# A planner that knows the delay between dependent neighbours, and convolution tiles placed after the following projection

## The chip, the cores and the metric

The kernel runs on one core of one Trainium2 chip. The metric is the device time of one execution in microseconds (us); lower is better. Five engines take part: TensorE (PE in the profile, its weight loads PEld), VectorE (DVE), ScalarE (ACT), GpSimd (POOL) and SyncE (SP, which only issues DMAs).

## The reference

A trunk of two layers over 512 tokens of width 1024, batch 1. Layer 0 mixes tokens with a gated linear recurrence and trailing means, layer 1 with a Conformer convolution module. Each layer then does cross-attention into 256 memory tokens and a gated MLP with a causal convolution of width 3. The change lies in layer 1's Conformer module and in the planner of the whole program:

```python
def conformer_conv(x, norm, w1, b1, dw_w, dw_b, ln_g, ln_b, w2, b2):
    h = rms_norm(x, norm) @ w1 + b1
    h = jax.nn.glu(h, axis=-1)
    h = causal_dwconv(h, dw_w, dw_b)
    h = jax.nn.silu(layer_norm(h, ln_g, ln_b))
    return h @ w2 + b2
```

`x` is 512 x 1024, `w1` 1024 x 2048, `w2` 1024 x 1024, all float32.

## The kernel before

Activations lie transposed, 128 channels on the partitions and 512 tokens along the free axis, so the width 1024 is eight tiles (`C = 8`). A float32 product is made of three matmuls in a reduced format (`mm3`, line 629): operands are split into a high and a low part (`split`, line 622: ACT copies the high part, DVE or POOL subtracts it), and a projection of one tile is 8 such triples, 24 matmuls of 128x512. A weight comes by an SP load into a 4 KB tile of the pool `w` (18 buffers) and is split into two more 4 KB tiles there, or, with `park=True`, into four 2 KB tiles of the pool `act` (48 buffers) (`load_w`, line 608).

**The planner.** No instruction is issued where it stands in the code. `Recorder` (line 201) collects every operation as a node with an estimated cost (`cost`, line 271), and `plan` (line 319) makes the order: first a backward pass (`late`, line 339) gives every node a due time, then a forward pass plays the engines and lets each take, whenever it is free, the first node that is ready: PE in program order, within a window of 60 nodes (`PE_WINDOW`), the others by due time. Buffers of the pools `act` and `w` go in the order of due times, those of the PSUM pools and of `tmp` in program order. The result is a fixed order for each engine and for SP's queue. A node on the same engine as the one it depends on is taken to be ready the moment that one ends; in the backward pass it is put down with the hop of another engine.

**The Conformer module** (`conformer`, line 1340). For each channel tile c: `project` with the second half of w1 gives the gate (ACT sigmoid, `gate`), `project` with the first half gives the value, and `gated` (line 1357) multiplies them on DVE into a buffer h (three of them in turn) and issues four SP DMAs that copy h into four `stacked` tiles, each with four shifted copies of 32 channels. `spread` (line 1369, POOL) prepares the filter taps as small matrices. `conv_pe` (line 1379) does the first taps of the convolution on PE, as float32 tiles of 128x32: 2 groups of 4 tiles for c = 0 to 6, 8 groups for c = 7. They accumulate in a PSUM buffer of the pool `aux`, of which there are two. `conv` (line 1396) adds the rest of the 31 taps: for c = 0 to 6 four on POOL (with ACT) and 19 on DVE, each a `scalar_tensor_tensor` that reads and writes the same PSUM buffer; c = 7 has none left. `merge` (line 1416) joins the parts with the bias and sets the PSUM buffer free.

In program order the loop's step c is: gate projection of tile c+1, `spread(c + 1)`, `conv_pe(c)`, value projection and `gated(c + 1)`, the weights of tile c+2, `conv(c)`. In the last step the attention's `mem.keys(4)` stands in the place of the gate projection. Behind the loop comes the layer norm over channels: sums over PE (`quarters`, `total`), squares, the root of the variance on ACT (`spread_scale`, line 767), then for each tile a multiply on DVE, Silu on ACT and a split. Work for the following cross-attention that needs nothing of this chain (`mem.values(0)`, `mem.values(1)`, `mem.keys(5)` to `mem.keys(7)`) stands behind it in program order, so PE can take it while it waits. Then `project_all` multiplies with the first three tiles of w2, loaded by `load_w(I["pw2"][n])`, all three side by side.

The feed-forward stages (line 978) take about half of the span. They are issued through the same planner; their code isn't touched.

Of the kernel before, what the change touches and what calls it, by code (L numbers as in the profile page):

```python
# [12 lines left out]
F32 = mybir.dt.float32  # L13
F32R = mybir.dt.float32r
AF = mybir.ActivationFunctionType
ALU = mybir.AluOpType

P = 128
# [3 lines left out]
C = D // P  # L22
# [14 lines left out]
PE_GROUPS = [2, 2, 2, 2, 2, 2, 2, 8]  # L37
N_POOL = [4] * 7 + [0]
LAG = 5
PLAIN = 3  # L40

KE = 4
# [140 lines left out]
class Node:  # L183

    def __init__(self, index, eng):
        self.index, self.eng, self.calls, self.us, self.tail = index, eng, [], 0.0, 0.0
        self.table, self.port, self.lat = None, False, 0.0
        self.before, self.after = set(), set()
        self.start = self.end = None


# [9 lines left out]
class Recorder:  # L201
# [4 lines left out]
    PATIENCE = 40.0  # L206
    WIRE = 0.83 / (256 * 1024)
    LAND = {"SP": 1.9, "ACT": 1.9, "POOL": 2.3}

    def __init__(self, tc):  # L210
        self.tc, self.nc = tc, tc.nc
# [35 lines left out]
    def touch(self, node, v, write):  # L247
        t = v.tile
        lo, hi, mask, _ = v.region()
        if t.psum:  # L250
            lo, hi, mask = 0, 127, 1
        if not t.nodes:
            self.tiles.append(t)
        if not t.nodes or t.nodes[-1] is not node:
            t.nodes.append(node)

        def meets(e):
            return e[0] <= hi and lo <= e[1] and e[2] & mask

        for e in t.writes + (t.reads if write else []):  # L260
            if meets(e) and e[3] is not node:
                node.before.add(e[3])
        if write:
            keep = lambda e: not (lo <= e[0] and e[1] <= hi and (e[2] & mask) == e[2])
            t.writes = [e for e in t.writes if keep(e)]
            t.reads = [e for e in t.reads if keep(e)]
            t.writes.append((lo, hi, mask, node))
        else:
            t.reads.append((lo, hi, mask, node))

    def cost(self, node, eng, method, args, how, reads):
        out = args[0]
        n = int(np.prod((reads[0] if not isinstance(out, View) else out).shape[1:]))
        if method == "dma_start":
            src = out if isinstance(out, View) else reads[0]
            node.tail += self.WIRE * 4 * n * src.shape[0] * (1.9 if "accum_op" in how else 1)
            window = any(k[0] == "window" for k in src.steps) or any(k[0] == "window" for r in reads for k in r.steps)
            node.us += 0.65 if window else {"SP": 0.42, "ACT": 0.42, "POOL": 0.6}[eng]
            return
        if eng == "PE":  # L280
            node.lat = 0.17
            if method == "transpose":
                node.us += 0.11
            elif out.shape[0] == 32:
                node.us += 0.875 / 4
            else:
                plain = args[1].tile.dtype == F32
                node.us += max(0.11, 0.0133 + n / 2400.0) * (4 if plain and n > 128 else 1)
            return
        wide = max([n] + [int(np.prod(r.shape[1:])) for r in reads[:1]])  # L290
        sources = [r for r in reads if int(np.prod(r.shape[1:])) > 4]
        node.port = node.port or eng == "POOL" and method != "memset"
        if eng == "ACT":
            node.lat = 0.1
            node.us += 0.1 + wide * 0.00083
            if isinstance(how.get("bias"), View):
                node.us += 0.06
            if "accum_out" in how:
                node.us += 0.2
            f = args[2]  # L300
            if f not in (AF.Copy, AF.Identity, AF.Square):
                node.table = f
        elif eng == "DVE":
            node.lat = 0.08
            node.port = node.port or len(sources) > 1 and not any(r.tile.psum for r in sources)
            if method == "reciprocal":
                node.us += 0.07 + wide * 0.00625
            elif method == "tensor_tensor_scan":
                node.us += 0.12 + wide * 0.002
            elif method == "scalar_tensor_tensor":  # L310
                node.us += 0.12 + wide * 0.00106
            else:
                node.us += 0.07 + wide * 0.001046
        else:
            node.lat = 0.06
            slow = method == "tensor_tensor" and how["op"] == ALU.mult
            node.us += 0.1 + n * (0.001 if method == "memset" else 0.0033 if slow else 0.0023)

    def plan(self):
# [19 lines left out]
        def late(extra):  # L339
            for o in reversed(nodes):  # L340
                due = end if o.ideal is None else o.ideal + o.us
                for a in list(o.after) + extra.get(o, []):
                    due = min(due, a.due - self.HOP - o.lat - (o.tail + self.LAND[o.eng] + self.SAFE if o.tail else 0.0))
                o.due = due - 1.15 * o.us

        def turn(t):
# [27 lines left out]
        ready = {e: [] for e in ("PE", "ACT", "DVE", "POOL", "SP")}  # L374
# [21 lines left out]
        while done < len(nodes):  # L396
# [11 lines left out]
            for e, r in ready.items():  # L408
# [4 lines left out]
                for i, (_, _, o) in enumerate(r):  # L413
# [21 lines left out]
                    us = o.us  # L435
# [15 lines left out]
                    del r[i]  # L451
                    done += 1
                    heapq.heappush(soon, (o.end, o.index, "end", o))
                    hop = lambda a: now + us if a.eng == o.eng and not o.tail else o.end + self.HOP
                    for a, at in [(a, hop(a)) for a in o.after] + [(a, now) for a in opens.get(o, [])]:
                        wait[a] -= 1
                        a.at = max(getattr(a, "at", 0.0), at)
# [52 lines left out]
def trunk(ctx: ExitStack, tc: tile.TileContext, I: dict, out_t: bass.AP, out: bass.AP):  # L510
# [23 lines left out]
    def nm(s):  # L534
        uid[0] += 1
        return f"{s}_{uid[0]}"
# [18 lines left out]

    def aux_ps():
        return aux.tile([P, T], F32, tag="aux", name=nm("aux"))

    wide = [True, 0]

# [21 lines left out]
    def col(name, i=0):  # L582
        j = _COL[name] + i
        return par[:, j : j + 1]
# [58 lines left out]
    class Norm:  # L643
        due = None
# [119 lines left out]
        V.reciprocal(r, sd)  # L764
        return r

    def spread_scale(s, weight):

        ps = stat_ps()
        for j in range(4):  # L770
            PE.matmul(ps[:, j : j + 1], s[:, j * P : (j + 1) * P], weight[:, :1], start=True, stop=True)
        rt = small.tile([P, 4], F32, tag="rtok", name=nm("rtok"), bufs=2)
        A.activation(rt, ps[:, :4], AF.Sqrt, bias=eps)
        V.reciprocal(rt, rt)
        d = tmp_f()
        V.tensor_tensor(
            d.rearrange("p (a b) -> p a b", a=4), ident.unsqueeze(1).broadcast_to([P, 4, P]),
            rt.unsqueeze(2).broadcast_to([P, 4, P]), op=ALU.mult,
        )
        out = aux_ps()  # L780
        PE.matmul(out, unit, d, start=True, stop=True)
        return out

    def project(w, i, xs):
        ps = mm_ps()
        for k in range(C):
            mm3(ps, blk(w, k * P), xs[k], k == 0, k == C - 1)
        if Norm.due:
            Norm.due.r = rstd(Norm.due.ss)
            Norm.due = None  # L790
        return ps
# [548 lines left out]
    def conformer(norm, nxt, mem, parked):  # L1340
        fold = small.tile([P, 32], F32, tag="fold", name="fold", bufs=1)
        V.tensor_reduce(fold, ident.rearrange("p (a b) -> p a b", b=4), axis=mybir.AxisListType.X, op=ALU.add)
        hs, outs = [None] * C, []

        def gate(c, psb):
            b = tmp_f()
            A.activation(b, psb, AF.Sigmoid, bias=col("c_b_pw1", C + c))
            return b

        def pieces(c):  # L1350
            return load_w(I["pw1"][C + c], V if c == 2 else G), load_w(I["pw1"][c], G)
# [84 lines left out]
        gated(0, gate(0, ps[0]), ps[1])  # L1436
        w = w[2:]
        mu = stat_ps()
        for c in range(C):
            if c < C - 1:  # L1440
                b = gate(c + 1, project(w[0], c + 1, norm.x))
                spread(c + 1)
            else:
                mem.keys(KE)
            conv_pe(c)
            if c < C - 1:
                gated(c + 1, b, project(w[1], c + 1, norm.x))
                if c < C - 2:
                    w = pieces(c + 2)
            else:  # L1450
                mem.eng = G
                ready = [mem.piece(i, park=True) for i in range(4)] + [mem.piece(i) for i in range(4, 8)]
            conv(c)
        merge(*pend.pop())
        mean = total(mu, aux_ps())
        var, sqs = aux_ps(), []
# [5 lines left out]
                quarters(var, sqs)  # L1462
        f = tmp_f()
        A.activation(f, var, AF.Copy)
        r = spread_scale(f, fourth)
        xs = []
        for c in range(C):
            V.tensor_tensor(outs[c], outs[c], r, op=ALU.mult)
            f = act_f()
            A.activation(f, outs[c], AF.Silu, scale=col("c_ln_g", c), bias=col("c_ln_b", c))  # L1470
            xs.append(split(f))
        mem.values(0, ready[:4])
        mem.values(1, ready[4:])
        for n in range(KE + 1, C):
            mem.keys(n)
        mem.eng = None

# [3 lines left out]
            V.scalar_tensor_tensor(X[n], ps, col("c_b_pw2", n), X[n], op0=ALU.add, op1=ALU.add)  # L1481
            nxt.feed(n)

        w = [load_w(I["pw2"][n]) for n in range(3)]
        for n, ps in enumerate(project_all(w, xs)):
            finish(n, ps)
        for n in range(3, C):
# [116 lines left out]
```

## Time and profile before

| | us |
|---|---|
| median of 3 runs | 1433.64 |
| lowest, highest | 1433.30, 1433.87 |
| the profiled execution's own time | 1433.83 |
| its span, first to last instruction | 1432.0 |
| PE busy in the span | 1421.8 |
| DVE busy | 1223.8 |
| ACT busy | 853.2 |
| POOL busy | 185.3 |

The granted clock of PE is 1.000 over the span. The Conformer module runs from about 735 to 910 us. Where the profile says that PE is busy, matmuls are in flight; a tile that waits inside a block shows in the length of the block more than in PE's idle time. All operations go through one line of the recorder, L498, so groups are told apart by their tiles' names: `mm`, `aux` and `stat` are PSUM buffers, `h` is the gated tile, `actf` a 2 KB tile, `wf` a raw weight, `wr` a 4 KB split operand, `tmp` a temporary. In a timeline row stand the start, the length of the merged row, the engine and the operation with its count, and in brackets the idle time before it and who ended it. Rows of one engine overlap by the pipeline's length, so the pace of a series is its length less that of one operation, over the count less one.

### The profile page before, as it was taken

The numbers are of one execution on the slowest core, as the hardware profiler recorded it, in microseconds if no ns is written. First come the engines' busy times: TensorE is split into PE (matmuls) and PEld (weight loads), VectorE is DVE, ScalarE is ACT, GpSimd is POOL, SyncE is SP. The second block draws the span as 40 slices with busy tenths as digits, with TensorE's granted clock in tenths as the row PEclk, the third lists the DMA queues.
The fourth block names the chain that finished last, engine by engine and source line by source line (L and its number), as shares of the span: only waits on it lengthen the run. The fifth ranks groups of instructions, "written<-read, shape, count | busy, mean of one in ns | idle before, by whom it ended". The sixth has DMA issues, their size and how long they took to land. (4 is left out here: it accounts for less than half of the span.)

```text
span 1432.0 us, 20240 instructions
## 1 busy us (share of the span) xinstructions
PE 1421.8 (99%) x7512; PEld 1199.9 (84%) x7512; DVE 1223.8 (85%) x1874; ACT 853.2 (60%) x1298; POOL 185.3 (13%) x196
## 2 busy tenths in 40 slices
PE   9999999999999999999999999999999999999998
PEld 8888888888988888888886676888898888888888
DVE  8986964758999999999967996776699999999996
ACT  8578854446866566656643436654577665666654
POOL 0000000001111010110006663300011111011000
PEclk9999999999999999999999999999999999999999
DMA  9332322228877786886515572322688777787821
GB/s 349 104 103 74 123 96 90 76 86 224 234 205 209 208 215 188 216 211 178 166 57 136 134 230 75 118 84 79 175 230 213 205 192 221 205 222 181 216 90 60
DMA packets 75988, 231.91 MB, mean 162 GB/s; under 512 B 8561, under 2 KB 10609, under 8 KB 75889
## 3 DMA queue, kind: packets, MB, share of 16 engines
q1 hardware_dynamic: 61488, 192.20, 40.7%
q0 software_dynamic: 13824, 37.75, 15.6%
q8 instruction: 59, 0.97, 0.3%
q10 hardware_dynamic: 576, 0.67, 0.1%
q14 instruction: 41, 0.33, 0.1%
HBM read 207.52 MB, written 2.10 MB: 146 GB/s over the span
## 5 line engine op out<-in xcount | busy, mean ns | idle before, releaser
L498 PE MATMUL mm<-act,wr 128*128 128x512 f32 (+1 forms) x4599 | 987.3, 368 | 1.7 <-ACT tmp L498 1.0
L498 PEld LDWEIGHTS mm<-act,wr 128*128 128x128 f32 x4599 | 802.1, 188 | 155.2 <-issue 5.8
L498 ACT ACTIVATE wr<-wf 128x1024 fp32r<-128x1024 f32 x295 | 308.4, 1053 | 116.8 <-PE mm L498 27.0
L498 DVE TENSOR_TENSOR wr<-wf,wr 128x1024 fp32r<-128x1024 f32 x272 | 329.4, 1219 | 37.3 <-ACT wr L498 18.7
L498 PE MATMUL aux<-act,wr 128*128 128x512 f32 (+1 forms) x1509 | 293.7, 337 | 0.1
L498 PEld LDWEIGHTS aux<-act,wr 128*128 128x128 f32 x1509 | 232.6, 190 | 28.8 <-ACT tmp L498 0.5
L498 ACT ACTIVATE tmp<-aux 128x512 f32<-128x512 f32 (+1 forms) x189 | 107.5, 571 | 94.8 <-PE aux L498 93.6
L498 DVE TENSOR_TENSOR tmp<-tmp,tmp 128x512 f32<-128x512 f32 (+1 forms) x151 | 99.4, 658 | 10.1 <-ACT tmp L498 6.3
L498 POOL DMA_DIRECT2D wf<-in_wup x48 | 42.7, 889 | 500.9 <-ACT act L498 275.9
L498 DVE TENSOR_TENSOR x<-x,mm 128x512 f32<-128x512 f32 (+1 forms) x126 | 81.5, 648 | 22.3 <-PE mm L498 21.6
L498 DVE SCALAR_TENSOR_TENSOR aux<-h,par,aux 128x497 f32<-128x497 f32 (+18 forms) x133 | 93.1, 731 | 4.7 <-PE aux L498 2.1
L498 POOL DMA_DIRECT2D wf<-wf x48 | 41.5, 864 | 382.0 <-PE mm L498 129.7
L498 ACT ACTIVATE act<-tmp 128x512 fp32r<-128x512 f32 (+1 forms) x85 | 52.9, 627 | 59.5 <-DVE tmp L498 59.4
L498 ACT ACTIVATE act<-actf 128x512 fp32r<-128x512 f32 (+1 forms) x136 | 70.0, 536 | 28.4 <-DVE actf L498 26.4
L498 PE MATMUL aux<-act,act 128*128 128x256 f32 (+1 forms) x456 | 84.4, 327 | 0.0
L498 PEld LDWEIGHTS aux<-act,act 128*128 128x128 f32 x456 | 73.7, 189 | 11.4 <-ACT tmp L498 0.5
L498 DVE TENSOR_TENSOR act<-actf,act 128x512 fp32r<-128x512 f32 (+1 forms) x136 | 76.0, 583 | 1.7 <-ACT act L498 1.5
L498 DVE SCALAR_TENSOR_TENSOR tmp<-h,par,tmp 128x512 f32<-128x512 f32 x96 | 72.0, 750 | 5.3 <-ACT tmp L498 2.7
L498 ACT ACTIVATE tmp<-h,par 128x512 f32<-128x512 f32 (+3 forms) x69 | 52.6, 782 | 31.2 <-DVE h L498 30.9
L498 POOL TENSOR_TENSOR wr<-wf,wr 128x1024 fp32r<-128x1024 f32 x23 | 55.1, 2406 | 91.2 <-PE mm L498 42.2
L498 DVE TENSOR_TENSOR tmp<-mm,tmp 128x512 f32<-128x512 f32 x84 | 57.1, 685 | 6.4 <-PE mm L498 6.1
L498 DVE TENSOR_TENSOR act<-tmp,act 128x512 fp32r<-128x512 f32 (+1 forms) x85 | 57.6, 682 | 0.4 <-ACT act L498 0.2
(150 smaller groups left out, 1067.2 us busy)
## 6 DMA issues: line engine op xcount, KB each, us to landing
wf<-in_wup SPq DMA_DIRECT2D x144, 512.0 KB, 4.8
wf<-in_wup POOLq DMA_DIRECT2D x48, 512.0 KB, 5.7
wf<-in_wdown SPq DMA_DIRECT2D x48, 512.0 KB, 5.3
actf<-in_wup SPq DMA_DIRECT2D x48, 256.0 KB, 6.3
wf<-wf POOLq DMA_DIRECT2D x48, 256.0 KB, 6.0
wf<-in_pw SPq DMA_DIRECT2D x24, 512.0 KB, 4.0
wf<-in_win SPq DMA_DIRECT2D x20, 512.0 KB, 3.6
wf<-in_wk SPq DMA_DIRECT2D x16, 512.0 KB, 5.9
```

The source lines that it names most:

```text
L498: getattr(eng, method)(*[real(a) for a in args], **{k: real(v) for k, v in how.items()})
```

## The change

- **Planner.** `DRAIN` gives a delay of 0.12 us on DVE and 0.2 us on ACT. In the forward pass a node that reads what the node before it on the same engine wrote (`feeds`) is ready only after that delay. In the backward pass a successor on the same engine is put down with that delay (none on PE and POOL) in place of the hop and latency.
- **Costs.** A DMA of shifted copies is estimated at 0.8 us of issue in place of 0.65 and twice the transfer time; a convolution tile at 0.225 us in place of 0.219, and 0.06 us more where it starts an accumulation.
- **Order in the Conformer loop.** `AFTER = 2`: the loop goes by half steps (a projection each), and `conv_pe(c)` with `conv(c)` now stand behind both projections of tile c+1 in place of behind the first. At the end `mem.keys(4)` and `mem.keys(5)` both stand ahead of `conv_pe(7)`; the keys behind the layer norm are 6 and 7.
- **Function tables.** `table` issues an ACT operation on one column, once with Sqrt, after all sigmoids and ahead of the root, and once with Silu, after the root and ahead of the first Silu.
- **Three weights.** The first three tiles of w2 are loaded with `park=True`.

```diff
@@ Recorder.touch
             if meets(e) and e[3] is not node:
                 node.before.add(e[3])
+                if not write:
+                    e[3].feeds.add(node)
@@ Recorder.cost
+            node.tail *= 2.0 if window else 1.0
-            node.us += 0.65 if window else {"SP": 0.42, "ACT": 0.42, "POOL": 0.6}[eng]
+            node.us += 0.8 if window else {"SP": 0.42, "ACT": 0.42, "POOL": 0.6}[eng]
...
-                node.us += 0.875 / 4
+                node.us += 0.9 / 4 + (0.06 if how["start"] else 0.0)
@@ plan, late
-                    due = min(due, a.due - self.HOP - o.lat - (o.tail + self.LAND[o.eng] + self.SAFE if o.tail else 0.0))
+                    if a.eng == o.eng and not o.tail:
+                        due = min(due, a.due - self.DRAIN.get(o.eng, 0.0))
+                    else:
+                        due = min(due, a.due - self.HOP - o.lat - (o.tail + self.LAND[o.eng] + self.SAFE if o.tail else 0.0))
@@ plan, forward
-                    hop = lambda a: now + us if a.eng == o.eng and not o.tail else o.end + self.HOP
+                    drain = self.DRAIN.get(o.eng, 0.0)
+                    same = lambda a: now + us + (drain if a in o.feeds else 0.0)
+                    hop = lambda a: same(a) if a.eng == o.eng and not o.tail else o.end + self.HOP
@@ trunk
+    def table(f, behind):
+        w = A.activation(small.tile([P, 1], F32, tag="warm", name=nm("warm"), bufs=1), eps, f)
+        w.before.update(behind)
+        return w
@@ spread_scale
+        w = table(AF.Sqrt, gates) if gates else None
+        root = A.activation(rt, ps[:, :4], AF.Sqrt, bias=eps)
+        if gates:
+            root.before.add(w)
+            gates.append(root)
@@ conformer
-        for c in range(C):
-            if c < C - 1:
-                b = gate(c + 1, project(w[0], c + 1, norm.x))
-                spread(c + 1)
+        for i in range(2 * C - 2 + AFTER):
+            c = i // 2 + 1
+            if i >= 2 * C - 2:
+                mem.keys(KE + i - 2 * C + 2)
+            elif i % 2 == 0:
+                b = gate(c, project(w[0], c, norm.x))
+                spread(c)
             else:
-                mem.keys(KE)
-            conv_pe(c)
-            if c < C - 1:
-                gated(c + 1, b, project(w[1], c + 1, norm.x))
-                if c < C - 2:
-                    w = pieces(c + 2)
-            else:
+                gated(c, b, project(w[1], c, norm.x))
+                if c < C - 1:
+                    w = pieces(c + 1)
+            if i == 2 * C - 2:
                 mem.eng = G
...
-            conv(c)
+            c = i + 1 - AFTER
+            if c >= 0 and c % 2 == 0:
+                conv_pe(c // 2)
+                conv(c // 2)
...
+            w = None if c else table(AF.Silu, gates[-1:])
+            silu = A.activation(f, outs[c], AF.Silu, scale=col("c_ln_g", c), bias=col("c_ln_b", c))
+            if c == 0:
+                silu.before.add(w)
...
-        for n in range(KE + 1, C):
+        for n in range(KE + AFTER, C):
             mem.keys(n)
...
-        w = [load_w(I["pw2"][n]) for n in range(3)]
+        w = [load_w(I["pw2"][n], park=True) for n in range(3)]
```

More of the change, by code (lines that the diff above doesn't have):

```diff
@@ L39 @@
 LAG = 5
+AFTER = 2
 PLAIN = 3
@@ L187, in __init__ @@
         self.table, self.port, self.lat = None, False, 0.0
-        self.before, self.after = set(), set()
+        self.before, self.after, self.feeds = set(), set(), set()
         self.start = self.end = None
@@ L208 @@
     LAND = {"SP": 1.9, "ACT": 1.9, "POOL": 2.3}
+    DRAIN = {"DVE": 0.12, "ACT": 0.2}
     def __init__(self, tc):
@@ L765, in scale_of, with spread_scale @@
         return r
-    def spread_scale(s, weight):
+    def spread_scale(s, weight, gates=None):
         ps = stat_ps()
@@ L772, in spread_scale @@
         rt = small.tile([P, 4], F32, tag="rtok", name=nm("rtok"), bufs=2)
-        A.activation(rt, ps[:, :4], AF.Sqrt, bias=eps)
+        w = table(AF.Sqrt, gates) if gates else None
[3 more added lines that the diff above has]
+            gates.append(root)
         V.reciprocal(rt, rt)
@@ L1342, in conformer @@
         V.tensor_reduce(fold, ident.rearrange("p (a b) -> p a b", b=4), axis=mybir.AxisListType.X, op=ALU.add)
-        hs, outs = [None] * C, []
+        hs, outs, gates = [None] * C, [], []
         def gate(c, psb):
             b = tmp_f()
-            A.activation(b, psb, AF.Sigmoid, bias=col("c_b_pw1", C + c))
+            gates.append(A.activation(b, psb, AF.Sigmoid, bias=col("c_b_pw1", C + c)))
             return b
@@ L1438, in conformer @@
         mu = stat_ps()
-        for c in range(C):
-            if c < C - 1:
-                b = gate(c + 1, project(w[0], c + 1, norm.x))
-                spread(c + 1)
-            else:
-                mem.keys(KE)
-            conv_pe(c)
-            if c < C - 1:
-                gated(c + 1, b, project(w[1], c + 1, norm.x))
-                if c < C - 2:
-                    w = pieces(c + 2)
-            else:
-                mem.eng = G
-                ready = [mem.piece(i, park=True) for i in range(4)] + [mem.piece(i) for i in range(4, 8)]
-            conv(c)
+        for i in range(2 * C - 2 + AFTER):
[5 more added lines that the diff above has]
+                spread(c)
+            else:
+                gated(c, b, project(w[1], c, norm.x))
+                if c < C - 1:
+                    w = pieces(c + 1)
+            if i == 2 * C - 2:
+                mem.eng = G
+                ready = [mem.piece(k, park=True) for k in range(4)] + [mem.piece(k) for k in range(4, 8)]
+            c = i + 1 - AFTER
+            if c >= 0 and c % 2 == 0:
+                conv_pe(c // 2)
+                conv(c // 2)
         merge(*pend.pop())
@@ L1464, in conformer @@
         A.activation(f, var, AF.Copy)
-        r = spread_scale(f, fourth)
+        r = spread_scale(f, fourth, gates)
         xs = []
@@ L1469, in conformer @@
             f = act_f()
-            A.activation(f, outs[c], AF.Silu, scale=col("c_ln_g", c), bias=col("c_ln_b", c))
+            w = None if c else table(AF.Silu, gates[-1:])
+            silu = A.activation(f, outs[c], AF.Silu, scale=col("c_ln_g", c), bias=col("c_ln_b", c))
+            if c == 0:
+                silu.before.add(w)
             xs.append(split(f))
```

## The prediction

> **What bounds the kernel now.** I read the page first (busy times, slices), then the stretches of 40 us, then PE's, DVE's and ACT's timelines of the Conformer module. The page:
>
> ```profile
> span 1432.0 us, 20240 instructions
> PE 1421.8 (99%) x7512; PEld 1199.9 (84%) x7512; DVE 1223.8 (85%) x1874; ACT 853.2 (60%) x1298; POOL 185.3 (13%) x196
> ```
>
> PE is busy for all but 10.2 us, at full clock (the rows below), so no edit that leaves the matmuls as they are can gain much: the prize is what PE loses in waits, idle or hidden inside busy blocks. The stretches say where (columns: PE, PEld, DVE, ACT, POOL busy, clock, DMA share, GB/s):
>
> ```profile
> 520.00:560.00 40.00, 39.52 (x211) 33.73 (x210) 38.31 (x56) 24.01 (x35) 4.36 (x5) 1.00 0.77 207
> 760.00:800.00 40.00, 38.76 (x182) 26.98 (x175) 37.30 (x53) 14.75 (x20) 25.27 (x20) 1.00 0.53 142
> 1200.00:1240.00 40.00, 39.52 (x211) 33.72 (x210) 39.02 (x58) 24.26 (x35) 5.05 (x6) 1.00 0.78 204
> ```
>
> The Conformer loop (from 760 us) loses PE time and has DVE nearly full; the feed-forward stages lose 0.48 us once each. PE's timeline of the loop, tile blocks (`aux<-actf,wf`) and what stands between:
>
> ```profile
> 738.64 20.58 PE L498 MATMUL mm<-act,wr 128*128 128x512 f32 x90
> 759.14 2.28 PE L498 MATMUL aux<-actf,wf 128*32 128x512 f32 x16
> 772.47 1.92 PE L498 MATMUL aux<-actf,wf 128*32 128x512 f32 x16
> 784.10 1.16 PE L498 MATMUL aux<-actf,wf 128*32 128x512 f32 x4
> 787.55 1.90 PE L498 MATMUL aux<-actf,wf 128*32 128x512 f32 x10 [0.98 <-DMA actf<-h]
> 814.84 1.06 PE L498 MATMUL aux<-actf,wf 128*32 128x512 f32 x6
> 816.23 1.90 PE L498 MATMUL aux<-actf,wf 128*32 128x512 f32 x10 [0.33 <-DMA actf<-h]
> 843.01 2.74 PE L498 MATMUL aux<-actf,wf 128*32 128x512 f32 x16
> 858.15 2.76 PE L498 MATMUL aux<-actf,wf 128*32 128x512 f32 x24
> 860.84 3.26 PE L498 MATMUL mm<-wr,wr 128*128 128x256 f32 x24
> 864.03 4.33 PE L498 MATMUL aux<-actf,wf 128*32 128x500 f32 x40
> 894.26 0.39 PE L498 MATMUL mm<-act,wr 128*128 128x512 f32 x1
> 895.26 2.93 PE L498 MATMUL mm<-act,wr 128*128 128x512 f32 x11 [0.61 <-DVE act L498]
> ```
>
> A block of 16 that waits for nothing takes 1.92 us (772.47). The block of c = 0 takes 2.28, c = 2 from 784.10 to 789.45 = 5.35, c = 4 from 814.84 to 818.13 = 3.29, c = 6 2.74. The excess is 0.36 + 3.43 + 1.37 + 0.82 = 5.98 us, most of it for the copies of h. A seventh microsecond goes at the end of the layer norm: after 894.26 the next matmul starts 1.00 us later, where it takes 0.23 (20.58 us for 90), so 0.77. So 5.98 + 0.77 = 6.75 us is all that the module can give back.
>
> **Why the blocks wait.** The row of h and that of the copies for c = 2:
>
> ```profile
> 777.89 0.75 DVE L498 SCALAR_TENSOR_TENSOR h<-mm,par,tmp 128x512 f32<-128x512 f32 x1
> 778.67 4.26 SPq L498 DMA_DIRECT2D actf<-h  x4
> ```
>
> From h (778.64) to the tile that waited last (787.55) pass 8.9 us: 4.3 of issuing and the landing of the last copy. One projection, 24 x 0.229 = 5.5 us, doesn't cover that; two, 11.0, do with 2.1 to spare. The change puts two between, so I cost the excess at zero afterwards; if h comes over 2.1 us late from DVE's queue, that cover is gone and the difference comes back. Where PE has something else ready the planner, which now puts the copies later by 4 x 0.15 us of issue and twice the transfer, will fill in with it.
>
> **But the stall may only move.** PE takes the later work (values, keys) as filler while the loop runs. What it doesn't lose at the blocks it will lose at 895 us, unless the chain that ends there ends sooner. That chain is DVE from the first tap, the layer norm, the first split. So the gain is the chain's shortening, up to 6.75 us. Its rows, groups of 761.4 to 866.3 us first:
>
> ```profile
> L498 DVE SCALAR_TENSOR_TENSOR aux<-h,par,aux 128x497 f32<-128x497 f32 (+18 forms) x133 | 93.1, 731 | 4.7 <-PE aux L498 2.1
> L498 DVE SCALAR_TENSOR_TENSOR actf<-aux,par,actf 128x512 f32<-128x512 f32 x7 | 5.2, 746 | 0.0
> L498 DVE SCALAR_TENSOR_TENSOR h<-mm,par,tmp 128x512 f32<-128x512 f32 x7 | 5.2, 746 | 0.0
> ...
> 761.46 2.30 DVE L498 SCALAR_TENSOR_TENSOR aux<-h,par,aux 128x500 f32<-128x500 f32 x3 [2.15 <-PE aux L498]
> 764.33 13.66 DVE L498 SCALAR_TENSOR_TENSOR aux<-h,par,aux 128x497 f32<-128x497 f32 x18
> 848.44 6.44 DVE L498 SCALAR_TENSOR_TENSOR aux<-h,par,aux 128x486 f32<-128x486 f32 x10
> 854.79 0.75 DVE L498 SCALAR_TENSOR_TENSOR actf<-aux,par,actf 128x512 f32<-128x512 f32 x1
> 865.63 0.75 DVE L498 SCALAR_TENSOR_TENSOR actf<-aux,par,actf 128x512 f32<-128x512 f32 x1
> ```
>
> *DVE's pace.* The 18 taps at 764.33 all belong to c = 0, each reading what the one before wrote: (13.66 - 0.73) / 17 = 0.76 us apart. The 10 at 848.44 alternate between two tiles: (6.44 - 0.72) / 9 = 0.636. A dependent neighbour costs 0.125 us. With none, the stretch would take 133 x 0.636 + 14 x 0.66 (7 merges, 7 h: 0.746 less the same overlap) + 1.2 (a weight's split, as at 893.39 below) = 95.0; it takes 866.38 - 761.46 = 104.9. So 9.9 us, or 79 taps, are lost to it. The planner will now alternate wherever two accumulators are live. It can't elsewhere, and there are two: the first tile is alone until the second block, two projections and a block later (11.0 + 1.9 = 12.9 us, 16 taps); the last for at least its second half (11); and at each of five changes the next block waits for the merge (0.75), the product PE has in hand (0.7) and itself (1.92): 3.4 us, 4 to 5 taps, 22 in all. 49 remain, 30 go: 3.7 us. Bounds: 0 (no new pair) and 9.9.
>
> *Its start.* The 90 matmuls ahead of the first block are 48 of c = 0, 24 of the gate and already 18 of the 24 that the change puts ahead. Six more are 6 x 0.229 = 1.4 us; at most the whole 5.5, if other work slips in too. The h of c = 1 moves ahead of the taps (-0.7). Net +0.7 us. DVE ends 3.0 us sooner, at 863.4.
>
> *The last block.* The layer norm starts after z of c = 7: block to 868.36, then ACT (868.43, quoted below). A block of keys, 3.26 us, stands inside it now. After the change it can start when the merge of c = 5 frees its accumulator (855.5, now 852.5) plus 0.7, and takes 2.76 + 4.33 = 7.1: 860.3, or 863.6 with keys inside. With ACT's 0.7 that is at most 864.3, where DVE gives 863.4. I take 864.0 against 869.1 now: 5.1 sooner; bounds -4.0 (third rival) to 11.9 (no keys inside, DVE at its upper bound of 9.9 - 0.7).
>
> *Tables, and the three weights.* ACT and DVE at the end of the layer norm:
>
> ```profile
> 868.43 0.69 ACT L498 ACTIVATE actf<-aux,par 128x512 f32<-128x512 f32 x1 [0.32 <-PE aux L498]
> 884.11 1.28 ACT L498 ACT_TABLE_LOAD   x1
> 885.40 0.26 ACT L498 ACTIVATE rtok<-stat,eps 128x4 f32<-128x4 f32 x1
> 888.75 1.28 ACT L498 ACT_TABLE_LOAD   x1
> 890.05 0.81 ACT L498 ACTIVATE actf<-actf,par 128x512 f32<-128x512 f32 x1
> 891.58 1.06 ACT L498 ACTIVATE wr<-wf 128x1024 fp32r<-128x1024 f32 x1 [0.72 <-PE mm L498]
> 892.55 0.61 ACT L498 ACTIVATE act<-actf 128x512 fp32r<-128x512 f32 x1
> ...
> 883.89 0.94 PE L498 MATMUL stat<-fourth,tmp 128*128 128x1 f32 x8
> 889.07 3.08 DVE L498 TENSOR_TENSOR actf<-actf,aux 128x512 f32<-128x512 f32 x5 [0.79 <-PE aux L498]
> 893.39 1.22 DVE L498 TENSOR_TENSOR wr<-wf,wr 128x1024 fp32r<-128x1024 f32 x1
> 894.52 1.29 DVE L498 TENSOR_TENSOR act<-actf,act 128x512 fp32r<-128x512 f32 x2
> ```
>
> The sums are ready at 884.83, the root starts at 885.40: 0.57 us less with the table there. The first multiply ends at 889.75 (0.68 in), Silu starts at 890.05: 0.3 less. Together 0.85 (0 to 0.87). Two operations on one column are added, at most 0.26 each (the root's row). The first waits for all sigmoids and comes while ACT is idle; the second waits for the root, and behind it in ACT's queue stand copies of the values' results, 1.5 us later, for which PE doesn't wait as long as it has filler. The w2 weights are split in the middle of this chain: ACT's 1.06 us ahead of 892.55, DVE's 1.22 ahead of 894.52. A parked weight needs one 4 KB buffer where it needed three, so it can come before the chain; I take 1.1 us, one of the two (0 to 2.2).
>
> The Trainium skill, ScalarE: Activation LUTs, "What ACT_TABLE_LOAD costs", adds about 1.38 us of drain to the same 1.28 for a switch of sets. By it the two would be worth up to 2.8 us more; the trace disagrees: the root starts 0.01 us after the load.
>
> *Sum.* 5.1 + 0.85 + 1.1 = 7.05, cut to the 6.75 there are. PE comes to its filler's weights some 6 us earlier, and each has to be loaded and split by then; in the stretch 738 to 900 us ACT waits for loads of w1 alone 19.1 us, since on SP's queue they stand behind four copies that wait for h:
>
> ```profile
> L498 ACT ACTIVATE wr<-wf 128x1024 fp32r<-128x1024 f32 x21 | 22.1, 1054 | 33.0 <-DMA wf<-in_pw 19.1 <-DVE wr L498 8.5 <-DMA wf<-in_wk 4.2
> ```
>
> I deduct 1.5 us, an estimate: a load's late landing or two (ACT's share is 1.05 us). The rest of the program is re-planned as well. There DVE is as full and PE at 100%: only the two gaps of 0.48 us can close, and others can open. I take 0, bounds -2 and +2. So 5.25 us: 1432.0 - 5.25 = 1426.75 of span; what lies around it is 1433.83 - 1432.0 = 1.83; 1428.6, and the median stands 0.2 below the profiled execution: **1428.4 us**.
>
> **Rivals.**
> - *The stall moves, nothing goes* (22%). PE already puts blocks back by itself, DVE gets no new pairs (0 for 3.7) and a key block stays inside the last block. Layer norm +0.7, tables -0.85, weights -0.55: 1432.9. For it: alternation is there already at 848.44. Against: 79 lost taps. The Trainium skill, VectorE: DVE Perf Modes, "The DRAIN you can't avoid", backs this case: the pipe is flushed after every operation, chained or not, so order would save nothing. The trace disagrees: 0.636 and 0.76 us apart.
> - *Everything falls into place* (13%). All 6.75, and the feed-forward stages give 1.5 through the same delay on DVE: 1433.64 - 8.25 = 1425.4.
> - *Slower: two key blocks inside the last one* (12%). Key 5 now stands ahead of `conv_pe(7)` and PE goes by program order: if its weights land while the tiles run, another 3.26 us goes into the block that the layer norm waits for. With the late start and no new pairs: 3.26 + 0.7 - 0.85 = 3.1, so 1436.7. It decides if the second key's weights arrive after the last block has begun; if before, keys are filler and it costs nothing.
>
> **How the numbers follow.** Forecast 53%, rivals 22, 13 and 12. About 0.2% (2.9 us) is what a measurement of this kernel tells from no change, so faster means below 1430.8 and slower above 1436.5. Of the forecast nine tenths lie below (48), with the 13 and 2 of the first rival 63%; slower is the last rival less what stays below 1436.5, 10%; the rest 27%. The range 1425.0 to 1435.0 holds the forecast's bounds, the second rival and most of the first.
>
> **What would show it.** Right: blocks of c = 0 to 6 near 1.92 us each, no wait for `actf<-h`; longer runs of taps 0.636 apart, the last merge near 863; one root right behind its sums; no `wr<-wf` between Silu and split; the first w2 matmul near 889 to 890. Wrong: new PE idle time before 890 with a weight as releaser, or keys inside the block of c = 7.

## The result, and the profile after

| | us |
|---|---|
| before, median of 5 runs | 1433.6 (1433.3 to 1433.87) |
| changed, median of 5 runs | 1421.49 (1421.2 to 1423.64) |
| ratio, 95% interval | 0.992 (0.9907 to 0.9934) |
| profiled execution, its span | 1422.47, 1420.7 |

12.1 us or 0.8% faster; 5.25 were forecast, and the range ended at 1425.0. The page of the changed kernel:

```profile
span 1420.7 us, 20240 instructions
PE 1413.3 (99%) x7512; PEld 1200.4 (84%) x7512; DVE 1206.1 (85%) x1877; ACT 846.7 (60%) x1304; POOL 186.2 (13%) x196
```

The number of instructions is equal; the durations of DVE's operations add up to as much as before (1328.6 us against 1328.7), but DVE is busy 17.7 us less, since more of them overlap. To see where the time went, the same stages have to be compared. I cut both traces at the same matmuls: the last transposes of layer 0's attention, the product with the unit matrix (`aux<-tmp,unit`) ahead of the Conformer module and the one in its layer norm, the last transposes of layer 1's attention, the first sums behind the last norm. That gives the first feed-forward stage, the Conformer module up to its layer norm, the rest of it with the second attention, and the second feed-forward stage. Stretches of the kernel before (length, busy PE, PEld, DVE, ACT, POOL, clock, DMA share, GB/s):

```profile
318.03:734.91 416.88, 416.29 (x2257) 359.97 (x2256) 391.26 (x594) 263.87 (x395) 42.59 (x53) 1.00 0.72 198
734.91:888.02 153.11, 151.53 (x778) 106.44 (x777) 125.52 (x186) 64.23 (x93) 85.38 (x57) 1.00 0.46 131
888.02:1014.42 126.40, 125.79 (x636) 106.30 (x634) 86.67 (x134) 67.78 (x115) 12.03 (x5) 1.00 0.29 98
1014.42:1424.04 409.62, 409.02 (x2280) 356.28 (x2279) 382.12 (x590) 255.01 (x388) 41.67 (x48) 1.00 0.69 186
```

And of the changed kernel:

```profile
317.70:732.52 414.82, 414.82 (x2258) 360.38 (x2257) 385.38 (x594) 260.92 (x395) 45.00 (x54) 1.00 0.74 199
732.52:878.21 145.69, 145.69 (x772) 104.76 (x770) 117.57 (x185) 64.16 (x94) 82.88 (x56) 1.00 0.50 141
878.21:1004.51 126.30, 126.30 (x640) 107.39 (x639) 91.76 (x137) 67.37 (x120) 13.19 (x5) 1.00 0.28 94
1004.51:1412.79 408.28, 407.64 (x2281) 356.66 (x2280) 375.62 (x590) 252.23 (x388) 41.53 (x48) 1.00 0.70 186
```

The stages gave 2.06, 7.42, 0.10 and 1.34 us, 0.33 came earlier: 11.25 of span. In the first three PE is now busy for the whole stage. The counts of matmuls (778 and 636 before, 772 and 640 after) show that a few moved between the second and the third stage, so their 7.42 and 0.10 us are best read as 7.5 together. The prediction had given the module 5.25 and the feed-forward stages nothing.

Now the module, PE's timeline of the changed kernel (start, length, operation, count):

```profile
761.50 1.92 PE L508 MATMUL aux<-actf,wf 128*32 128x512 f32 x16
771.09 1.92 PE L508 MATMUL aux<-actf,wf 128*32 128x512 f32 x16
784.09 1.92 PE L508 MATMUL aux<-actf,wf 128*32 128x512 f32 x16
798.44 1.92 PE L508 MATMUL aux<-actf,wf 128*32 128x512 f32 x16
811.43 1.92 PE L508 MATMUL aux<-actf,wf 128*32 128x512 f32 x16
826.67 1.89 PE L508 MATMUL aux<-actf,wf 128*32 128x512 f32 x16
839.40 1.92 PE L508 MATMUL aux<-actf,wf 128*32 128x512 f32 x16
854.22 6.89 PE L508 MATMUL aux<-actf,wf 128*32 128x512 f32 x64
878.67 7.00 PE L508 MATMUL mm<-wr,wr 128*128 128x512 f32 x51
885.51 1.55 PE L508 MATMUL mm<-act,act 128*128 128x512 f32 x6
```

No block waits (before: up to 5.35 us), no keys stand inside the last one, and the first w2 matmul (885.51, both operands in `act` now) follows the work before it directly. DVE's timeline of the same kernel:

```profile
763.49 7.71 DVE L508 SCALAR_TENSOR_TENSOR aux<-h,par,aux 128x500 f32<-128x500 f32 x10 [3.12 <-PE aux L508]
784.92 12.32 DVE L508 SCALAR_TENSOR_TENSOR aux<-h,par,aux 128x491 f32<-128x491 f32 x19
840.17 12.31 DVE L508 SCALAR_TENSOR_TENSOR aux<-h,par,aux 128x491 f32<-128x491 f32 x19
854.99 6.06 DVE L508 SCALAR_TENSOR_TENSOR aux<-h,par,aux 128x489 f32<-128x489 f32 x8
861.29 0.74 DVE L508 SCALAR_TENSOR_TENSOR actf<-aux,par,actf 128x512 f32<-128x512 f32 x1
```

Runs of 19 taps are now (12.31 - 0.72) / 18 = 0.644 us apart, where the runs before held 0.76; only at the two ends of the loop (763.49, 854.99: (6.06 - 0.72) / 7 = 0.763) is a tile alone. From first tap to last merge DVE takes 98.5 us in place of 104.9.

### The profile page after: what moved, and what is told of

It reads as the page before. It is cut to its first block, busy times and chain, and to the rows that moved or that the text cites. A ratio compares the mean times of both kernels' runs of the same rounds, so it can differ in the third digit from the quotient of the medians.

```text
span 1420.7 us, 20240 instructions
## 1 busy us (share of the span) xinstructions
PE 1413.3 (99%) x7512; PEld 1200.4 (84%) x7512; DVE 1206.1 (85%) x1877; ACT 846.7 (60%) x1304; POOL 186.2 (13%) x196
## 4 chain that ended last, share of the span: by engine, by line
PE 99%; DMA 1%; ACT 0%; DVE 0%; DVEq 0%; issue 0%; POOL 0%; POOLq 0%
PE mm L508 70%; PE aux L508 27%; PE stat L508 1%; DMA actf<-in_wup 1%; ACT wr L508 0%; DVE wf L508 0%; DVEq L1624 0%; ACT act L508 0%; ACT tmp L508 0%; ACT rtok L508 0%; DVE rtok L508 0%; POOL onesf L588 0%; POOL eps L588 0%; DVEq L508 0%; POOLq L1616 0%
## 5 line engine op out<-in xcount | busy, mean ns | idle before, releaser
L508 PE MATMUL mm<-act,wr 128*128 128x512 f32 (+1 forms) x4551 | 975.5, 368 | 0.0
L508 PEld LDWEIGHTS mm<-act,wr 128*128 128x128 f32 x4551 | 792.5, 188 | 147.6 <-issue 5.4
L508 ACT ACTIVATE wr<-wf 128x1024 fp32r<-128x1024 f32 x292 | 303.9, 1053 | 109.2 <-PE mm L508 40.8
L508 PE MATMUL aux<-act,wr 128*128 128x512 f32 (+1 forms) x1485 | 286.5, 335 | 0.6 <-ACT tmp L508 0.6
L508 PEld LDWEIGHTS aux<-act,wr 128*128 128x128 f32 x1485 | 229.5, 190 | 28.1 <-ACT tmp L508 1.0
L508 POOL DMA_DIRECT2D wf<-wf x48 | 41.3, 861 | 409.3 <-DMA wf<-in_wup 151.4
L508 DVE SCALAR_TENSOR_TENSOR aux<-h,par,aux 128x500 f32<-128x500 f32 (+18 forms) x133 | 88.2, 727 | 3.9 <-PE aux L508 3.1
L508 PE MATMUL aux<-act,act 128*128 128x256 f32 (+1 forms) x480 | 91.0, 330 | 0.0
L508 PEld LDWEIGHTS aux<-act,act 128*128 128x128 f32 x480 | 78.3, 189 | 11.8
L508 DVE TENSOR_TENSOR act<-actf,act 128x512 fp32r<-128x512 f32 (+1 forms) x136 | 79.2, 606 | 1.4 <-ACT act L508 1.2
L508 ACT ACTIVATE tmp<-mm 128x512 f32<-128x512 f32 (+1 forms) x58 | 33.3, 574 | 55.7 <-PE mm L508 55.6
```

The lines of the kernel that those rows point to most:

```text
L508: getattr(eng, method)(*[real(a) for a in args], **{k: real(v) for k, v in how.items()})
```

## The experiments

Times are medians, each ratio against runs of the kernel before on the same chip. The table has the stage lengths of each run's profiled execution, cut as above; the module and the second attention are one column, since filler moves between them.

| run | median | ratio, 95% interval | first feed-forward | module and attention | second feed-forward |
|---|---|---|---|---|---|
| before | 1433.6 | | 416.9 | 279.5 | 409.6 |
| changed | 1421.49 | 0.9907 to 0.9934 | 414.8 | 272.0 | 408.3 |
| e1_planner_only | 1423.07 | 0.9915 to 0.9948 | 414.8 | 274.1 | 407.4 |
| e2_order_only | 1436.13 | 1.0012 to 1.0031 | 416.9 | 281.7 | 409.4 |
| e3_after_1 | 1423.31 | 0.9918 to 0.9947 | 414.8 | 273.6 | 407.9 |
| e4_no_forward | 1435.98 | 1.0009 to 1.0028 | 416.6 | 282.3 | 409.2 |
| e5_old_late | 1422.68 | 0.9911 to 0.9944 | 414.8 | 273.3 | 407.4 |
| e9_dearer_taps | 1436.84 | 1.0017 to 1.0037 | 414.8 | 287.3 | 407.5 |
| e7_no_park | 1422.95 | 0.9913 to 0.9943 | 414.8 | 273.8 | 407.4 |
| e10_planner_park | 1422.31 | 0.9908 to 0.9938 | 416.1 | 272.2 | 407.4 |
| e13_mean_taps | 1430.32 | 0.9969 to 0.9988 | 416.9 | 278.1 | 409.3 |
| e11_delay_double | 1421.97 | 0.9902 to 0.9935 | 414.9 | 272.4 | 407.5 |
| e1b_forward_only | 1424.79 | 0.9922 to 0.9952 | 414.8 | 275.5 | 407.4 |
| e6_no_tables | 1421.04 | 0.9898 to 0.9928 | 414.8 | 272.0 | 407.4 |

The shortest stage lengths come back in run after run: 414.8, 272.0 and 407.4 are the stages with PE waiting for next to nothing. Against them the kernel before lost 2.1 + 7.5 + 2.2 = 11.8 us. The runs of the changed kernel scatter by 2.4 us, so differences under 2 us between it and the variants near it rest on the stage lengths, not on the medians. These come from one profiled execution of each kernel; the 416.1 of e10 and the 408.3 of the changed kernel, 1.3 and 0.9 us above the shortest, warn against reading less than that into one of them.

### Is it the planner or the order of the loop?

One kernel had the delay alone, the other the loop order alone; two more took one of them out of the changed kernel.

```diff
 # e1_planner_only: before, plus
+    DRAIN = {"DVE": 0.12, "ACT": 0.2}
...
+                if not write:
+                    e[3].feeds.add(node)
...
+                    if a.eng == o.eng and not o.tail:
+                        due = min(due, a.due - self.DRAIN.get(o.eng, 0.0))
...
+                    same = lambda a: now + us + (drain if a in o.feeds else 0.0)
```

> The kernel before with the delay between dependent neighbours in both passes of the planner, and nothing else: old costs, old loop order, no early tables, no parked weights. Theory A (the delay in the forward pass is what frees DVE): the feed-forward stages give back the 2.07 and 1.35 us that they gave in the changed kernel, the Conformer module 2 to 4 us through fewer dependent taps (fewer than 40 of 133 where 74 were), about 1427. Theory B (the feed-forward gain is an accident of another plan): feed-forward within 1 us of before, 1431 to 1435.

```diff
 # e2_order_only: before, plus
+AFTER = 2
...
+        for i in range(2 * C - 2 + AFTER):
...
+            c = i + 1 - AFTER
+            if c >= 0 and c % 2 == 0:
+                conv_pe(c // 2)
+                conv(c // 2)
...
-        for n in range(KE + 1, C):
+        for n in range(KE + AFTER, C):
```

> The kernel before with the loop by half steps (the tile blocks behind both projections, keys 4 and 5 ahead of the last block) and nothing else. Theory A: the waits inside the tile blocks vanish (blocks of 1.9 us), but DVE's chain of taps stays as long, so the wait comes out at the end of the layer norm: 1 to 3 us gained, 1430.5 to 1432.5, feed-forward unchanged. Theory B (the order of the loop is what the Conformer module gained by): 6 to 7.4 us gained, 1426 to 1427.5.

```diff
 # e3_after_1: changed kernel, with
-AFTER = 2
+AFTER = 1
```

> The changed kernel with AFTER = 1: the tile blocks again behind one projection and key 5 again behind the layer norm; everything else of the change stays. Theory A (both the delay and the order are needed): waits for the copies return inside the blocks, 2 to 5 us, 1424 to 1427. Theory B' (with the truer cost of the copies the planner moves the blocks back by itself): within 1 us of the changed kernel, 1421 to 1422.5.

```diff
 # e4_no_forward: changed kernel, with
-                    same = lambda a: now + us + (drain if a in o.feeds else 0.0)
+                    same = lambda a: now + us
```

> The changed kernel without the delay in the forward pass (a dependent neighbour is ready at once, as before); the backward pass keeps it, and the rest of the change stays. Theory A: the feed-forward gain of 3.4 us goes, dependent taps are back near 74, the chain is some 5 us longer, 1427 to 1431. Theory B: the feed-forward gain stays or shifts by 1 us, the Conformer module keeps at least 5 of its 7.4 us, 1421 to 1424.

The planner alone gives 10.2 of the 12.1 us, more than theory A had for it, and both feed-forward stages fall to their floor. The loop order alone makes the kernel slower (+2.9 us, interval 1.0012 to 1.0031), which no theory had, and so does the whole change without the forward delay (+2.7). With the planner, going back to one projection (e3) costs 1.6 us in the module (273.6 against 272.0). Its blocks don't wait for copies (each of 16 takes 1.9 us, and starts 10.9 us or more after its h is done), so theory A was wrong in that. Nor is it the truer cost of the copies that theory B' named: in e1, with the old order and the old costs, each block of 16 takes 1.9 us too. With the delay in both passes of the plan, PE holds the blocks back by itself.

Why is the order alone slower? PE's and DVE's timelines of e2, around the block of c = 4:

```profile
801.47 11.22 PE L499 MATMUL mm<-act,wr 128*128 128x512 f32 x48
816.62 3.35 PE L499 MATMUL aux<-actf,wf 128*32 128x512 f32 x16 [3.93 <-issue]
...
815.77 0.75 DVE L499 SCALAR_TENSOR_TENSOR actf<-aux,par,actf 128x512 f32<-128x512 f32 x1
```

PE stands still for 3.93 us. The row names no releaser, but the block starts 0.1 us after the merge of c = 2 has ended (815.77 + 0.75), and that merge frees the accumulator which c = 4 needs. As I read it, the plan, blind to the delay, took DVE's taps to be faster than they are and had put no filler there. The wait for the copies was replaced by one for the accumulator. The block itself then takes 3.35 us in place of 1.92, since the granted clock is 0.55 from 816.60 to 819.90 (more on this in the last section), and behind the layer norm PE waits 1.38 us for its output where it waited 0.61 before.

### Does DVE's saved time matter, or that the plan is true?

The delay does two things: DVE's taps alternate, and the plan knows how long DVE really takes. Three runs take these apart. Two make the three-operand operation dearer in the plan of the kernel before, with no reason to alternate; one doubles DVE's delay in the changed kernel.

```diff
 # e9_dearer_taps: before, with
-                node.us += 0.12 + wide * 0.00106
+                node.us += 0.24 + wide * 0.00106
 # e13_mean_taps: before, with
-                node.us += 0.12 + wide * 0.00106
+                node.us += 0.17 + wide * 0.00106
 # e11_delay_double: changed kernel, with
-    DRAIN = {"DVE": 0.12, "ACT": 0.2}
+    DRAIN = {"DVE": 0.24, "ACT": 0.2}
```

> The kernel before with 0.12 us more in the estimated cost of DVE's three-operand operation (the taps) and no delay, so that the plan is as slow as a run of dependent taps but has no reason to put another operation between. Theory A (the gain is DVE time saved by putting independent operations between): taps as dependent as before (65 to 85 of 133), no gain or up to 2 us, 1431.5 to 1436. Theory C (the gain comes from a plan that is truer to the chip, so that PE's order fits): the blocks no longer wait and the Conformer module gains 3 us or more, 1426 to 1430.5.

> The kernel before with 0.05 us more in the estimated cost of DVE's three-operand operation and no delay: the plan then has the mean pace that DVE had (0.71 us), without a reason to alternate. Theory A (DVE time saved by alternating): the Conformer module gains 2 us at most, its taps stay 60 or more dependent; the feed-forward stages may gain their 2.07 and 2.1 us, as with the dearer taps; 1428 to 1432. Theory C (a right mean is enough): Conformer 5 us or more, 1422 to 1426.

> The changed kernel with a delay of 0.24 us on DVE in place of 0.12. Theory A: alternation is the same, only lone runs of taps are planned too slow, so within 1.5 us of the changed kernel, 1421 to 1424. Theory C (the plan's truth decides): PE's blocks come late as with the dearer taps, DVE waits for them 3 us or more, 1425 to 1432.

Feed-forward and module part ways. The stretch of the first feed-forward stage in e9, columns as above:

```profile
318.07:732.88 414.81, 414.81 (x2257) 360.30 (x2256) 390.36 (x594) 263.94 (x395) 46.07 (x55) 1.00 0.73 198
```

DVE is as busy as before (390.36 against 391.26; 385.38 in the changed kernel), and still the stage is at its floor. So here the gain isn't DVE time: an estimate that is 0.12 us longer for the three-operand operations there (the small convolution in `up` above all) was enough; what it moved in the plan I didn't trace. The 0.05 us of e13 were not (416.9).

In the module e9 loses 7.8 us. DVE's waits from 760 to 880 us, and PE's row of the last block:

```profile
DVE aux L498 <- PE aux L498: 12.4, 6, 2.7
...
862.92 8.70 PE L498 MATMUL aux<-actf,wf 128*32 128x512 f32 x48 [5.36 <-DVE actf L498]
```

Six times DVE waits for a block, 12.4 us in all: the plan takes alternating taps for slow too, and PE puts too much filler ahead of the blocks. Ahead of the last one it stands for 5.36 us, until a merge on DVE (`actf`) sets an accumulator free. Its taps even alternate more than before (35 dependent pairs by their starts, and five more starts that came late through waits, where theory A had 65 to 85), and it is slower all the same; neither theory had that. With the right mean pace (e13) the module gains 1.4 us; that is theory A's answer (2 at most), though its feed-forward stages stayed slow. The doubled delay, which is wrong only for a tile alone, costs the module 0.4 us, as A had it. So a true mean alone is not enough, nor are alternating taps alone. That the module needs both, taps that alternate and a plan that knows the pace of either kind, fits all these runs, but isn't shown: no run has a plan that is true for each pair and doesn't alternate.

### The backward pass, the parked weights, the tables

```diff
 # e5_old_late: changed kernel, with
-                    if a.eng == o.eng and not o.tail:
-                        due = min(due, a.due - self.DRAIN.get(o.eng, 0.0))
-                    else:
-                        due = min(due, a.due - self.HOP - o.lat - (...))
+                    due = min(due, a.due - self.HOP - o.lat - (...))
 # e1b_forward_only: before, plus feeds, DRAIN and the forward pass of e1
```

> The changed kernel with the backward pass as before (hop and latency between neighbours on one engine); the forward delay and all the rest stay. If the forward pass is the cause: within 1.5 us of the changed kernel, 1420.5 to 1423, dependent neighbours as rare. If the due times carry a part: 1424 to 1430.

> The kernel before with the delay in the forward pass alone. If the forward pass is the whole cause, as its removal said: 1422 to 1425, Conformer 6 to 7 us, feed-forward about 2.07 and 2 us. If the backward pass is needed with it where order, costs and tables are old: 1426 to 1431.

```diff
 # e7_no_park: changed kernel, with
-        w = [load_w(I["pw2"][n], park=True) for n in range(3)]
+        w = [load_w(I["pw2"][n]) for n in range(3)]
 # e10_planner_park: e1_planner_only, with
-        w = [load_w(I["pw2"][n]) for n in range(3)]
+        w = [load_w(I["pw2"][n], park=True) for n in range(3)]
```

> The changed kernel with the first three w2 weights in 4 KB buffers again. If the parked form is worth what the prediction gave it (1.1 us): 1422 to 1423.5, with a wait of PE for a weight's split right after the layer norm. If it is idle: 1421 to 1422.

> The kernel before with the delay in both passes and the three parked weights; old loop order, old costs, no early tables. The planner alone left PE a wait of 1.06 us for a w2 weight's split behind the layer norm. If parking takes that wait away: 1421 to 1422.3, as fast as the whole change, so that the loop order, the costs and the tables add nothing on top. If the loop order is worth something of its own: 1422.5 to 1424.

```diff
 # e6_no_tables: changed kernel, with
-        r = spread_scale(f, fourth, gates)
+        r = spread_scale(f, fourth)
...
-            w = None if c else table(AF.Silu, gates[-1:])
...
-                silu.before.add(w)
```

> The changed kernel without the two early table loads. By the prediction's term 0.85 us come back on the chain of the layer norm; PE waits there only if the chain is bound, so 1421.5 to 1422.5; by the page's rule with the drain up to 2.8 us more, 1423 to 1425.

The forward pass alone brings 8.8 us (1433.59 to 1424.79), as its expectation had it, though module and attention give 4.0 of them (279.5 to 275.5) and not the 6 to 7 expected of the module. In the stage lengths the backward pass is worth 1.3 us of the module in the changed kernel (273.3 against 272.0) and 1.4 in the kernel before (275.5 against 274.1), nothing elsewhere. Parking is worth 1.8 and 1.9 us of the module (273.8 against 272.0, 274.1 against 272.2). What it takes away, on PE's timeline of e1 and of e7 without it:

```profile
888.08 0.50 PE L506 MATMUL aux<-act,wr 128*128 128x512 f32 x1 [0.89 <-DVE wr L506]
```

```profile
887.08 0.50 PE L508 MATMUL mm<-act,wr 128*128 128x512 f32 x1 [0.40 <-DVE wr L508]
```

PE waits for the split of a w2 weight (`DVE wr`) once the layer norm is done. The weight loads show more of it: from 735 to 905 us they wait 2.1 us for such splits (on DVE and ACT) in e1 and 2.2 in e7, and not at all in the changed kernel. With the planner and parking alone (e10) the module is within 0.2 us of the whole change; its first feed-forward stage lost 1.3 us in this execution, which no other variant near the changed kernel did. So the loop order, the truer costs and the tables add little together, yet e3, which has all but the order, is 1.6 us longer in the module than the changed kernel. The difference shows in the last block: in e3 a block of keys stands inside it (10.1 us from its first tile to its last), and the weight loads wait 1.2 us for the layer norm's output; in e1 and e10, with the old order and the old costs, it takes 6.9 us as in the changed kernel. So the old order loses 1.6 us beside the new costs and tables, and nothing that shows beside the old ones; which of them does it wasn't tried. The tables add nothing that shows: 272.0 with and without, 1421.04 without. None of the variants is clearly faster than the changed kernel.

## Why the prediction was wrong

**The cause of the block waits: right; the cure: not needed.** All blocks of 16 take 1.9 us, and the copies have their time. But the prediction counted on the second projection in between, and e1 does without it: there the blocks start 7.8 us or more after their h, and none waits.

**"The stall may only move": right.** e2 is that case, with the accumulator in the place of the copies and a longer wait at the end of the layer norm behind it.

**The prize, "all that the module can give back": mis-sized.** 6.75 us were counted; the module with the attention behind it gave back 7.5. The remaining 0.7 us lie in smaller waits that I didn't trace.

**The feed-forward stages, "I take 0": the step that failed.** "Only the two gaps of 0.48 us can close" came from PE's idle time in the stretches of 40 us. Before, the stages were 2.1 and 2.2 us longer than their shortest, and the changed kernel's execution gained 2.06 and 1.34 of it, 3.4 together, beyond the bound of 2. The place to see it is the weight loads, whose waits show what PE's idle time (0.59 of 416.88 us) doesn't. The waits of PEld before, from 330 to 730 us (total, times, longest):

```profile
PEld mm L498 <- ACT tmp L498: 2.1, 4, 0.9
PEld aux L498 <- ACT tmp L498: 0.5, 2, 0.3
PEld aux L498 <- DVE tmp L498: 0.3, 1, 0.3
```

The same question for the changed kernel has no row. In other runs too the sum goes with what the stage lost: 2.7 us of waits in e13 (2.1 lost), 1.9 in e4 (1.8), 1.4 in e10 (1.3), 0.3 in e9 (none). For the second stage it is 3.2 us before (1020 to 1400 us) and none in e1. What had been taken at nothing was thus PE waiting, mostly for copies on ACT (`tmp`), which the plans of e1 and e9, with more time for DVE in them, don't have. e9 shows that this needs no DVE time saved; whether the 5.9 us of DVE time that the changed kernel saves in the first stage help as well stays open.

**DVE's pace: right in kind, too small.** 3.7 us were forecast from 30 pairs, 4.4 with the h that moves ahead; the chain is 6.4 shorter (98.5 against 104.9), near what 52 pairs at 0.125 make (6.5). Of 73 dependent pairs by their starts (the prediction reckoned 79) 21 are left, 9 and 7 of them in the two lone runs quoted above; the changeovers, costed at 4 to 5 lone taps each, kept hardly any, for a merge, an h or the other tile's tap stands between. The start slipped more: the first tap stands 31.0 us behind the module's first mark in place of 26.6, 4.4 later where 1.4 was taken and 5.5 the bound; 111 matmuls of `mm<-act,wr` stand ahead of the first block in place of 90. Net the last merge is 2.0 us sooner, not 3.0.

**The last block: right in size, by luck.** Its z is ready at 861.87 (ACT's row at 861.18, below), 129.4 us behind the mark where it was 134.2: 4.8 sooner, 5.1 forecast; DVE's merge ends together with it. But the forecast's 864.0 went by a merge of c = 5 that ends 3.0 sooner, a block that therefore starts 5 us sooner, and keys that may still stand inside it. That merge ends 120.6 us behind the mark in both kernels, the block starts 1.5 us sooner, and the rest is that the keys (3.26 us) left the block.

**Tables and weights.** ACT's timeline of the changed kernel:

```profile
861.18 0.69 ACT L508 ACTIVATE actf<-aux,par 128x512 f32<-128x512 f32 x1 [3.76 <-PE aux L508]
876.24 0.26 ACT L508 ACTIVATE rtok<-stat,eps 128x4 f32<-128x4 f32 x1 [1.67 <-PE stat L508]
876.52 1.28 ACT L508 ACT_TABLE_LOAD   x1
880.67 0.82 ACT L508 ACTIVATE actf<-actf,par 128x512 f32<-128x512 f32 x1
```

The root starts right behind its sums, as forecast, the second table lies between root and Silu. But PE no longer waits for that chain, so the 0.85 us are worth nothing, as e6 shows. The weights were worth 1.8 where 1.1 was taken.

**"I deduct 1.5 us" for late weights: wrong.** PE is busy for 145.69 of 145.69 us, and from 735 to 905 us its weight loads wait for no load and no split of a weight.

**The rivals.** The first assumed that DVE gets no new pairs; it got some 50. The Trainium skill, VectorE: DVE Perf Modes, "The DRAIN you can't avoid", has the pipe flushed after every operation, chained or not, and lets one that is not held start earlier; the prediction took from it that order would save nothing. Yet alternating taps stand 0.644 us apart and lone ones 0.763 in the changed kernel too. The second came nearest, and still fell short: the feed-forward stages gave 3.4 us and not 1.5. The third didn't come: the last block has no keys inside. The risk it stood for was real, by another mechanism: half of the change is slower than none (e2, e4).

So forecast and result differ by 6.9 us: 3.4 for the feed-forward stages, 2.2 for the module (7.42 against 5.25), 0.4 for the other stages, 0.8 since the median lies 1.0 below the profiled execution where it was taken as 0.2, and 0.1 outside the stages.

## What to carry to other kernels

Where a planner fixes the order, its estimates are part of the kernel: a missing delay of 0.12 us between dependent neighbours cost 10 us, and an estimate that is too long can be as bad: 0.12 us more on every three-operand operation made the kernel before 3.5 us slower (e9). Put filler where the plan knows that an engine waits before moving code by hand; a hand-made order on an untrue plan only moved the wait. Size what can be gained by stage lengths between the same instructions and by the waits of the weight loads, not by PE's idle time alone.

## What the runs showed of the hardware

A short stop of PE can cost more than itself. Stretches of e4, cut inside the stop ahead of a block and inside the block, for c = 2 (a stop of 1.47 us) and for c = 4 (2.90 us):

```profile
785.80:787.30 1.50, 0.08 (x1) 0.00 (x0) 1.50 (x4) 1.06 (x1) 0.00 (x0) 1.00 0.72 270
787.40:789.20 1.80, 1.80 (x17) 0.42 (x17) 1.73 (x3) 0.00 (x0) 0.00 (x0) 1.00 0.64 198
816.80:819.60 2.80, 0.00 (x0) 0.00 (x0) 2.80 (x6) 0.43 (x1) 2.80 (x2) 0.96 0.00 0
819.70:823.00 3.30, 3.30 (x16) 0.61 (x16) 3.16 (x5) 0.00 (x0) 0.98 (x1) 0.54 0.00 0
```

After 1.47 us without matmuls the clock stayed at 1.00 and the block's stretch took 1.8 us; after 2.90 us it was granted 0.54 and the stretch took 3.3. So the longer stop cost 1.5 us more than its own length. The stop of 3.93 us in e2 did the same (0.55). The Trainium skill, TensorE: Matmul & The Clock Gate, "Part 1: The HAM clock gate", gives an idle window of about 3.4 us for this; here less was enough.

The second thing is the price of dependence on DVE, 0.12 us for a tap that reads what the one before wrote (0.763 less 0.644). It is small against an operation of 0.73 us, and some 50 fewer such pairs are about the 6.4 us by which the chain became shorter.
